# Weight parts of a feed-forward made by casting and accumulating DMAs instead of ScalarE and VectorE

## The chip, the cores and the metric

The kernel runs on one core of a Trainium2 chip. The metric is the device time of one execution in microseconds (us); less is better. Engines are named as in the profile: PE (matmul), PEld (its weight load), DVE (VectorE), ACT (ScalarE), POOL (GpSimd), SP (which issues the ordinary DMAs).

## The reference

An encoder layer is applied to two groups of 256 tokens of width 1024, with shared weights: layer norm, three branches (mLSTM, grouped-query attention with rotary positions, cross-attention to 256 memory tokens), a gated merge, an output projection with residual and norm, and a gated convolutional feed-forward with residual and norm. All is float32. The part that the change touches:

```python
def conv_ffn(x, w_ffn_up, ffn_conv_w, ffn_conv_b, w_ffn_down):
    u = dwconv_centred(x @ w_ffn_up, ffn_conv_w, ffn_conv_b)
    return (jax.nn.gelu(u[..., :D_FF]) * u[..., D_FF:]) @ w_ffn_down
```

`D_FF` is 2816, so `w_ffn_up` is 1024 x 5632 and `w_ffn_down` 2816 x 1024.

## The kernel before, in words

All 512 tokens are worked on at once; a PSUM tile is 128 x 512 float32. Every operand of a product is split into a high part and a low part in the matmul's format (float32r): the high part is the value cast to it, the low part is the value less the high part. A product is made of three matmuls: high by high, high by low, low by high (`mm3`, L120 to L122).

Weights come in chunks of 128 x 1024 (512 KB). A chunk is loaded by a DMA of the SP queue into one of three `raw` buffers (L95). ACT casts `raw` into `whi` (L108), DVE subtracts: `wlo = raw - whi` (L109). There are six `whi` and six `wlo` buffers (`NW`), taken in turn. For `w_ffn_up` a chunk is 8 pieces of 128 columns side by side, one for each k tile, and so in memory 1024 rows of 512 B; for `w_ffn_down` it is 128 rows of 4 KB.

The feed-forward has 22 blocks of 128 channels (`NF`), each with two up tiles, `ua` (gelu) and `ub` (gate). An up tile is 24 matmuls of 512 columns into one PSUM tile, out of four for dense products (`pd`). Then ACT reads the PSUM tile (L465) and DVE reads it twice (L468, L471) for the convolution over tokens; ACT applies gelu to `ua` (L1079); DVE multiplies the two into `hf` (L1083). The tiles of the first two blocks are made early, in two halves; the rest, 40 tiles, follow in order. The down product then runs over the 22 blocks; each chunk takes 24 matmuls into eight PSUM tiles at once (L1133 to L1135), and the split of `hf` into `hs` high and low (L82, L83) belongs to it. The last four blocks are done token tile by token tile, with the second norm between.

The code asks for chunks up to three jobs ahead (`LOOKAHEAD`). Each engine has its own list of instructions, whose order is fixed when the program is built; an engine that waits at one instruction does nothing behind it. Across engines only semaphores order the work.

Of the kernel before, what the change touches and what calls it, by code (L numbers as in the profile page):

```python
# [12 lines left out]
F32 = mybir.dt.float32  # L13
F32R = mybir.dt.float32r
# [7 lines left out]
T = 256            # tokens of one request group  # L22
NT = 512           # tokens of both groups
NTT = NT // P
HM = 4             # mLSTM heads
HA = 8             # attention heads
HC = 4             # cross-attention heads
# [7 lines left out]
MAX_EXP = 88.7      # its exponential is still finite  # L35

# columns of w_in
# [9 lines left out]
class Encoder:  # L47
# [27 lines left out]
    def split(self, src, name, scale=None):  # L75
        """src = hi + lo exactly, both with 12 significant bits."""
        nc = self.nc
        hi, lo = self.a(f"{name}h", F32R), self.a(f"{name}l", F32R)
        n = src.free_size()
        h, l = hi[:, :n], lo[:, :n]  # L80
        if scale is None:
            nc.scalar.copy(h, src)  # L82
            nc.vector.tensor_tensor(l, src, h.bitcast(F32), op=ALU.subtract)  # L83
        else:
            nc.scalar.activation(h, src, AF.Copy, scale=scale)
            nc.vector.scalar_tensor_tensor(
                l, src, scale, h.bitcast(F32), op0=ALU.mult, op1=ALU.subtract
            )
        return hi, lo
# [21 lines left out]

    def rsqrt(self, out, in_):
        self.nc.gpsimd.tensor_tensor(  # L113
            out, in_, self.mhalf.to_broadcast(list(in_.shape)), op=ALU.pow
        )

# [7 lines left out]
    def stat(self, chunk, sub, x, evac, name, k0=0):  # L124
        """A job: out[128 columns of w, tokens] = w.T x; chunk() gives w's parts."""

        def run():
            wh, wl = chunk()
            ps = self.ps(name, dense=True)
            nk = wh.shape[1]  # L130
            c = slice(sub * P, sub * P + P)
            for k in range(nk):
                xh, xl = x[k0 + k]
                self.mm3(ps, wh[:, k, c], wl[:, k, c], xh, xl, k == 0, k == nk - 1)
            evac(ps)

        return run

    def chunk(self, *args):
        return Chunk(self, args)  # L140

    def add_stat(self, w, c0, ntile, x, evac, name):
        nk = len(x)
        per = max(1, 1024 // (nk * P))
        for i in range(ntile):
            if i % per == 0:
                ch = self.chunk(w, 0, nk, c0 + i * P, per * P)
            self.jobs.append(([ch], self.stat(ch.get, i % per, x, lambda p, i=i: evac(i, p), f"{name}{i}")))

    def add_nat(self, w, c0, ncol, x, evac, name):  # L150
        """Jobs for out[tokens, ncol columns], accumulated over chunks of two k tiles."""
        nk = len(x)
        box = {}
        for c in range(nk // 2):
            ch = self.chunk(w, 2 * c, 2, c0, ncol)

            def run(c=c, ch=ch):
                wh, wl = ch.get()
                for t in range(NTT):
                    if c == 0:  # L160
                        box[t] = self.ps(f"{name}{t}", dense=True)
                    ts = slice(t * P, t * P + P)
                    for kk in range(2):
                        k = 2 * c + kk
                        xh, xl = x[k]
                        mm = self.nc.tensor.matmul
                        o = box[t][:, :ncol]
                        mm(o, xh[:, ts], wh[:, kk, :], start=(k == 0), stop=False)  # L168
                        mm(o, xh[:, ts], wl[:, kk, :], start=False, stop=False)  # L169
                        mm(o, xl[:, ts], wh[:, kk, :], start=False, stop=(k == nk - 1))  # L170
                    if c == nk // 2 - 1:
                        evac(t, box[t])

            self.jobs.append(([ch], run))
# [11 lines left out]
    def run_jobs(self):  # L186
        """Runs the jobs (the chunks that they use, run) in order, with the chunks made ahead
        as the pool lets, and the side steps spread between them."""
# [26 lines left out]
    def constants(self):  # L215
# [11 lines left out]
        # masks over [s, t]: forward keeps s <= t, backward s >= t  # L227
# [10 lines left out]
    def late_constants(self):  # L238
        """Per-channel vectors as columns, and the rotary tables with the norm gains in them."""
# [14 lines left out]
        # head norm gain, with the halves of the output gate's sigmoid and of the merge gates'  # L254
# [31 lines left out]
    def norm_stats(self, y, tag="ln", bufs=2, st=None):  # L286
        """[mean, variance, -, 1 / deviation] of the rows y."""
        nc = self.nc
        if st is None:
            st = self.sm([P, 2, 6], "lnst")  # L290
            for h in range(2):
                nc.vector.bn_stats(st[:, h, :], y[h])
        mv = self.sm([P, 4], f"{tag}mv", bufs)
        nc.vector.bn_aggr(mv[:, 0:2], st.rearrange("p a b -> p (a b)"))
        nc.vector.tensor_scalar(mv[:, 2:3], mv[:, 1:2], EPS, None, op0=ALU.add)  # L295
        self.rsqrt(mv[:, 3:4], mv[:, 2:3])
        return mv

    def layer_norm(self, y, gb, st=None, share=False):
        """share: the second half on ScalarE and GpSimd."""  # L300
# [25 lines left out]
    def gain_rows(self, y, gb, halves=(0, 1)):  # L326
        """Gain and bias of rows, where nothing waits for them."""
# [15 lines left out]
    def turn_part(self, rows, ts, out, name, fs=(0, KT), affine=None):  # L343
        """Parts of the transpose of some adjacent token tiles, into out[k tile]; affine:
        the columns of gains and biases to apply."""
# [32 lines left out]
    def attend(self, heads, qparts, kparts, v, hT):  # L378
        """Steps for some heads over both groups, as a pipeline of (head, group) units.
        qparts(h) makes and kparts(h) gives parts of the transposed queries and keys,  # L380
        v(h, g, kt) parts of [128 keys, 128]; parts of 0.5 * the output, transposed, go to hT."""
# [103 lines left out]
    def ev_vog(self, b):  # L485
        """Blocks of 384 | 328 | 328 of the columns v 512 | o 512 | g 16."""
        def f(t, ps):
# [11 lines left out]
            # forward gates beside zeros, and zeros beside backward gates  # L499
# [14 lines left out]
    def mlstm_steps(self, qk, hT):  # L514
        """qk[i]: twice silu of the convolved q (i < 4) and k heads, [128, tokens]."""
# [4 lines left out]
        def rows():  # L520
            # gate rows by (direction, head), each in its own direction's time order
# [10 lines left out]
            # scans restart at each chunk  # L532
# [20 lines left out]
            # the running maximum, less bl  # L553
# [3 lines left out]
            # weights into the state (first chunk) and of the state (second chunk)  # L557
# [26 lines left out]
        def flipped():  # L584
# [8 lines left out]
            # the negated maximum as rows by (tile, direction, head), for all partitions  # L593
# [6 lines left out]
        def colq(q, d, t):  # L600
            """[128, 4 heads] of quantity q, direction d, token tile t."""
# [78 lines left out]
        def out(t, h):  # L680
            g, c = t // 2, t % 2
            ds = 0 if c == 1 else 1     # the direction with a state before this chunk
# [74 lines left out]
    def ev_rope(self, parts):  # L757
        """parts: (column, heads, table, sink, (mul, add)) of a natural block."""
# [45 lines left out]
    def build(self):  # L804
# [34 lines left out]
        # memory keys and values  # L839
# [17 lines left out]
        with self.tc.manual_schedule(engines=engines):  # L857
            # the tensor engine is kept busy, so that its clock is up, until the first rows arrive
# [54 lines left out]
        # cross-attention queries, attention inputs  # L913
# [57 lines left out]
        # merge of the branches, one branch at a time  # L971
# [20 lines left out]
        def branch(n, w, hT, nk, first, last, name, flush=False):  # L992
# [6 lines left out]
            if flush:  # L999
                # the first gates cover the last steps of what the branch waits for  # L1000
# [12 lines left out]
        # mLSTM inputs  # L1013
# [24 lines left out]
        # output projection, first residual and norm  # L1038
# [31 lines left out]
        # gated convolutional feed-forward  # L1070
# [15 lines left out]
        # the first tiles of the product for one group while the other group's rows are made  # L1086
# [29 lines left out]
        for f in range(EARLY, NF):  # L1116
            if f == NF - 1:
                self.add(lambda: [down_split(z) for z in range(3)])
            self.add_stat(w_up, f * P, 1, x2s, ev_up(f, 0), f"ua{f}")
            self.add_stat(w_up, DFF + f * P, 1, x2s, ev_up(f, 1), f"ub{f}")  # L1120
# [16 lines left out]
        dn = [self.chunk(w_dn, f, 1, 0, D) for f in range(NF)]  # L1137
# [38 lines left out]
class Chunk:  # L1176
    """Parts of a block of weights (w, first k tile, k tiles, first column, columns), made once."""

    def __init__(self, enc, args):
        self.enc, self.args, self.raw, self.parts = enc, args, None, None  # L1180

    def load(self):
        if self.raw is None:
            self.raw = self.enc.load_chunk(*self.args)

    def get(self, pieces=1):
        if self.parts is None:
            self.load()
            self.parts = self.enc.split_chunk(self.raw, self.args[2], self.args[4], pieces)
# [4 lines left out]
class LazyPair:  # L1194
    """The parts of a tile that is made later."""
# [22 lines left out]
def _rope_table():  # L1218
    """[token, (cos, sin), dim], the sines signed for x * cos + swapped x * sin."""
# [30 lines left out]
```

## Time and profile before

| | us |
|---|---|
| times of two executions | 953.58, 955.25 |
| median | 954.41 |
| profiled execution: span from first to last instruction | 951.1 |
| what lies around the span, by the two times | 2.5 to 4.1 |
| PE busy in it | 937.3 (99%) |
| DVE busy | 555.5 (58%) |
| ACT busy | 377.9 (40%) |
| POOL busy | 106.8 (11%) |

The profile is one execution. Its page gives no time of its own for it beside the span, so the span stands against the two times. A busy PE means that a matmul is in its pipeline; matmuls overlap, so the distance between their starts tells their rate, not the length of one. A stage is read by its own window, not by the shares of the whole span. The stages here: late up tiles (blocks 10 to 21, 24 tiles) from 693 to 823 us, down product from 823 us to the end.

### The profile page before, as it was taken

The page shows a single profiled execution, that of the slowest core. Times are in us where ns is not written, and L with a number is a line of the kernel's source. Part 1 is how long each engine was busy: PE and PEld are TensorE (multiplying, and loading weights), DVE is VectorE, ACT ScalarE, POOL GpSimd, SP SyncE. Part 2 cuts the span into 40 slices and gives each one's busy share as a digit, 9 for nine tenths or more (in the row PEclk, how much of TensorE's full clock was granted, in tenths as well). Part 3 has the DMA queues.
Part 4 walks back from the last instruction along what each step waited for, and adds up shares of the span by engine and source line. Part 5 has one row for each costly group of instructions (what it writes and reads, how often), then busy time and mean ns, then how long its engine had stood idle before and what let it go on. Part 6 is the DMA issues. An engine that isn't in the chain of part 4 may idle for free.

```text
span 951.1 us, 12119 instructions
## 1 busy us (share of the span) xinstructions
PE 937.3 (99%) x4654; PEld 795.3 (84%) x4654; DVE 555.5 (58%) x1006; ACT 377.9 (40%) x677; POOL 106.8 (11%) x99
## 2 busy tenths in 40 slices
PE   9989999999999999999999999999999999999996
PEld 7878888888889997888878889988888888888885
DVE  4674444896777435457668567755555555752217
ACT  4652543434555444344344313533433333542101
POOL 0160100440000000111019001000000000000004
PEclk9999999999999999999999999999999999999998
DMA  8354223224111253432253523333333333242202
GB/s 291 100 163 114 85 67 89 72 63 132 51 46 44 68 141 92 143 99 78 80 201 97 155 67 89 111 90 110 89 93 107 89 106 94 89 155 89 88 1 89
DMA packets 121485, 95.76 MB, mean 101 GB/s; under 512 B 3664, under 2 KB 105812, under 8 KB 121428
## 3 DMA queue, kind: packets, MB, share of 16 engines
q1 hardware_dynamic: 121428, 94.99, 33.1%
q8 instruction: 37, 0.61, 0.3%
q14 instruction: 20, 0.16, 0.1%
HBM read 92.86 MB, written 2.11 MB: 100 GB/s over the span
## 4 chain that ended last, share of the span: by engine, by line
PE 87%; DVE 3%; POOL 2%; issue 0%; DMA 0%; ACT 0%; DVEq 0%; POOLq 0%; SPq 0%; ACTq 0%
PE dn L1135 4%; PE dn L1133 4%; PE dn L1134 4%; PE ua L120 4%; PE ub L120 4%; PE ua L121 4%; PE ub L121 4%; PE ub L122 4%; PE ua L122 4%; PE ga L120 2%; PE vog L169 2%; PE vog L170 2%; PE vog L168 2%; PE ga L121 2%; PE ba L120 2%; PE ga L122 2%
## 5 line engine op out<-in xcount | busy, mean ns | idle before, releaser
L109 DVE TENSOR_TENSOR wlo<-raw,whi 128x1024 fp32r<-128x1024 f32 (+3 forms) x162 | 194.9, 1206 | 274.5 <-ACT whi L108 274.3
L108 ACT CAST whi<-raw 128x1024 fp32r<-128x1024 f32 (+3 forms) x162 | 163.2, 1012 | 360.3 <-PE ua L121 72.0
L113 POOL TENSOR_TENSOR lnmv<-lnmv,mhalf 128x1 f32<-128x1 f32 x8 | 7.7, 965 | 403.5 <-DVE lnmv L295 403.5
L400 ACT ACTIVATE prob<-sc,nmax 128x256 f32<-128x256 f32 x48 | 22.5, 476 | 24.6 <-DVE nmax L396 24.5
L113 POOL TENSOR_TENSOR rss<-rss,mhalf 128x4 f32<-128x4 f32 (+1 forms) x12 | 22.3, 1859 | 75.9 <-DVE rss L779 75.9
L1079 ACT ACTIVATE up<-up 128x512 f32<-128x512 f32 x22 | 13.9, 633 | 42.4 <-DVE up L471 42.4
L329 POOL TENSOR_TENSOR y<-y,gain 128x512 f32<-128x512 f32 x11 | 18.4, 1678 | 15.8 <-ACT y L319 15.8
L396 DVE TENSOR_REDUCE nmax<-sc 128x2 f32<-128x512 f32 x24 | 16.4, 681 | 4.3 <-PE sc L122 4.3
L330 POOL TENSOR_TENSOR y<-y,gain 128x512 f32<-128x512 f32 x11 | 17.3, 1579 | 0.5
L83 DVE TENSOR_TENSOR probTl<-pt,probTh 128x512 fp32r<-128x512 f32 x24 | 16.4, 682 | 1.4 <-ACT probTh L82 1.4
L1083 DVE TENSOR_TENSOR hf<-up 128x512 f32<-128x512 f32 x22 | 15.2, 692 | 0.9
L465 ACT ACTIVATE up<-ub,col 128x512 f32<-128x512 f32 x20 | 15.6, 778 | 0.0
L465 ACT ACTIVATE up<-ua,col 128x512 f32<-128x512 f32 x20 | 15.5, 777 | 0.0
L986 DVE SCALAR_TENSOR_TENSOR gate<-gate,ba 128x512 f32<-128x512 f32 x8 | 5.5, 686 | 17.2 <-PE ba L122 9.2
L471 DVE SCALAR_TENSOR_TENSOR up<-ub,col,up 128x510 f32<-128x510 f32 x20 | 15.0, 748 | 0.7
L471 DVE SCALAR_TENSOR_TENSOR up<-ua,col,up 128x510 f32<-128x510 f32 x20 | 15.0, 748 | 0.7
L406 DVE TENSOR_SCALAR prob<-prob,rsum 128x256 f32<-128x256 f32 x48 | 14.8, 351 | 0.8
L82 ACT CAST probTh<-pt 128x512 fp32r<-128x512 f32 x24 | 14.0, 583 | 2.4 <-PE pt L417 1.9
L468 DVE SCALAR_TENSOR_TENSOR up<-ua,col,up 128x510 f32<-128x510 f32 x20 | 14.9, 743 | 0.0
L468 DVE SCALAR_TENSOR_TENSOR up<-ub,col,up 128x510 f32<-128x510 f32 x20 | 14.9, 743 | 0.0
L417 PE MATMUL pt<-ident,prob 128*128 128x128 f32 x96 | 14.7, 274 | 0.0
L319 ACT ACTIVATE y<-y,lnmv 128x512 f32<-128x512 f32 x3 | 2.4, 816 | 27.7 <-DVE lnmv L322 27.7
(1460 smaller groups left out, 2953.3 us busy)
## 6 DMA issues: line engine op xcount, KB each, us to landing
raw<-in_w_in SPq DMA_DIRECT2D x48, 512.0 KB
raw<-in_w_ffn_up SPq DMA_DIRECT2D x44, 512.0 KB
raw<-in_w_ffn_down SPq DMA_DIRECT2D x22, 512.0 KB
raw<-in_w_mem_kv SPq DMA_DIRECT2D x8, 512.0 KB
raw<-in_w_branch_attn SPq DMA_DIRECT2D x8, 512.0 KB
raw<-in_w_out SPq DMA_DIRECT2D x8, 512.0 KB
raw<-in_w_in SPq DMA_DIRECT2D x8, 328.0 KB
raw<-in_w_branch_mem SPq DMA_DIRECT2D x4, 512.0 KB
```

Source lines behind the costliest of these rows:

```text
L108: nc.scalar.copy(hi[:, s], raw[:, s])
L109: nc.vector.tensor_tensor(lo[:, s], raw[:, s], hi[:, s].bitcast(F32), op=ALU.subtract)
L113: self.nc.gpsimd.tensor_tensor(out, in_, self.mhalf.to_broadcast(list(in_.shape)), op=ALU.pow)
L120: mm(ps, lh, rh, start=first, stop=False)
L121: mm(ps, lh, rl, start=False, stop=False)
L122: mm(ps, ll, rh, start=False, stop=last)
L465: nc.scalar.activation(y, ps, AF.Identity, bias=w[3], scale=w[1])
L468: nc.vector.scalar_tensor_tensor(y3[:, :, 1:T], p3[:, :, 0 : T - 1], w[0], y3[:, :, 1:T], op0=ALU.mult, op1=ALU.add)
L471: nc.vector.scalar_tensor_tensor(y3[:, :, 0 : T - 1], p3[:, :, 1:T], w[2], y3[:, :, 0 : T - 1], op0=ALU.mult, op1=ALU.add)
L1133: mm(o, xh[:, ts], wh[:, 0, cs], start=(f == 0), stop=False)
L1134: mm(o, xh[:, ts], wl[:, 0, cs], start=False, stop=False)
L1135: mm(o, xl[:, ts], wh[:, 0, cs], start=False, stop=(f == NF - 1))
```

## The change

Two other ways to make a chunk's parts are added, and a chunk is told which one it uses.

- `cast`, for the up tiles of blocks 10 to 21 (24 chunks): a DMA of the POOL queue loads the weights from memory straight into `whi`, cast on the way. ACT writes `wlo = -whi`. A second DMA of the POOL queue reads the same weights from memory again and adds them into `wlo`. No `raw` buffer is used.
- `sum`, for all 22 down chunks: SP loads `raw` as before, ACT casts it into `whi` and writes `wlo = -whi`, and a DMA of the POOL queue adds `raw` into `wlo`, from on-chip memory to on-chip memory.

All other chunks are made as before. Comments and docstrings are dropped too, and the line numbers of what stands behind the new functions grow by 30.

```diff
+    def cast_chunk(self, w, k0, nk, c0, ncol):
+        n = nk * ncol
+        hi = self.whl.tile([P, 1024], F32R, tag="hi", name="whi")
+        lo = self.whl.tile([P, 1024], F32R, tag="lo", name="wlo")
+        self.nc.gpsimd.dma_start(
+            hi[:, :n].rearrange("p (k c) -> p k c", k=nk), self.chunk_src(w, k0, nk, c0, ncol)
+        )
+        return hi, lo
+
+    def finish_cast(self, parts, w, k0, nk, c0, ncol):
+        nc = self.nc
+        hi, lo = [t[:, : nk * ncol] for t in parts]
+        nc.scalar.activation(lo, hi.bitcast(F32), AF.Copy, scale=-1.0)
+        view = lambda t: t.rearrange("p (k c) -> p k c", k=nk)
+        nc.gpsimd.dma_start(view(lo), self.chunk_src(w, k0, nk, c0, ncol), accum_op=ALU.add)
+        return [view(t) for t in (hi, lo)]
+
+    def sum_chunk(self, raw, nk, ncol):
+        nc = self.nc
+        n = nk * ncol
+        hi = self.whl.tile([P, 1024], F32R, tag="hi", name="whi")
+        lo = self.whl.tile([P, 1024], F32R, tag="lo", name="wlo")
+        nc.scalar.copy(hi[:, :n], raw[:, :n])
+        nc.scalar.activation(lo[:, :n], hi[:, :n].bitcast(F32), AF.Copy, scale=-1.0)
+        nc.gpsimd.dma_start(lo[:, :n], raw[:, :n], accum_op=ALU.add)
+        return [t[:, :n].rearrange("p (k c) -> p k c", k=nk) for t in (hi, lo)]
...
-            self.add_stat(w_up, f * P, 1, x2s, ev_up(f, 0), f"ua{f}")
-            self.add_stat(w_up, DFF + f * P, 1, x2s, ev_up(f, 1), f"ub{f}")
+            self.add_stat(w_up, f * P, 1, x2s, ev_up(f, 0), f"ua{f}", "cast" if f >= 10 else "vec")
+            self.add_stat(w_up, DFF + f * P, 1, x2s, ev_up(f, 1), f"ub{f}", "cast" if f >= 10 else "vec")
...
-        dn = [self.chunk(w_dn, f, 1, 0, D) for f in range(NF)]
+        dn = [self.chunk(w_dn, f, 1, 0, D, how="sum") for f in range(NF)]
...
     def get(self, pieces=1):
         if self.parts is None:
             self.load()
-            self.parts = self.enc.split_chunk(self.raw, self.args[2], self.args[4], pieces)
+            if self.how == "cast":
+                self.parts = self.enc.finish_cast(self.raw, *self.args)
+            elif self.how == "sum":
+                self.parts = self.enc.sum_chunk(self.raw, self.args[2], self.args[4])
+            else:
+                self.parts = self.enc.split_chunk(self.raw, self.args[2], self.args[4], pieces)
```

In POOL's list nothing stood between the norms before the feed-forward and those of the tail. Now, at the start of the late up chunks (numbers tell buffers apart; L119 is the casting DMA, L129 the accumulating one):

```order
L143 TENSOR_TENSOR lnmv_5467<-lnmv_5467,mhalf_91 128x1
L119 DMA whi_6233<-in_w_ffn_up 128x8x128
L129 DMA wlo_6234<-in_w_ffn_up 128x8x128
L119 DMA whi_6269<-in_w_ffn_up 128x8x128
L129 DMA wlo_6270<-in_w_ffn_up 128x8x128
L119 DMA whi_6304<-in_w_ffn_up 128x8x128
L119 DMA whi_6340<-in_w_ffn_up 128x8x128
L129 DMA wlo_6305<-in_w_ffn_up 128x8x128
L129 DMA wlo_6341<-in_w_ffn_up 128x8x128
L119 DMA whi_6375<-in_w_ffn_up 128x8x128
L129 DMA wlo_6376<-in_w_ffn_up 128x8x128
```

From the third chunk on the pattern cast, cast, add, add, cast, add repeats to the last up chunk; then the 22 adds of the down chunks (L139) follow one another.

ACT's list at the same place before (L108 the cast of a chunk, L465 the read of an up tile's PSUM, L1079 gelu):

```order
L1079 ACTIVATE up<-up 128x512
L108 CAST whi<-raw 128x1024
L465 ACTIVATE up<-ub_6166,col 128x512
L108 CAST whi<-raw 128x1024
L465 ACTIVATE up<-ua_6203,col 128x512
L1079 ACTIVATE up<-up 128x512
```

and now (L127 the negation, L495 and L1109 what L465 and L1079 were):

```order
L1109 ACTIVATE up<-up 128x512
L127 ACTIVATE wlo<-whi 128x1024
L495 ACTIVATE up<-ub_6166,col 128x512
L127 ACTIVATE wlo<-whi 128x1024
L495 ACTIVATE up<-ua_6203,col 128x512
L1109 ACTIVATE up<-up 128x512
```

The negation stands where the cast stood, one chunk for one up tile; it now waits for the landing of the cast DMA of the chunk that is used six tiles after the tile read just before it.

## Rows read from the trace of the kernel before

**Rows 1.** Page: span, busy us and shares; the clock in 40 slices, in tenths.

```profile
span 951.1 us, 12119 instructions
...
PE 937.3 (99%) x4654; PEld 795.3 (84%) x4654; DVE 555.5 (58%) x1006; ACT 377.9 (40%) x677; POOL 106.8 (11%) x99
...
PEclk9999999999999999999999999999999999999998
```

**Rows 2.** Waits of PE: waiting line, releaser, us in total, times, longest; all.

```profile
PE xT3p L357 <- ACT affine L367: 1.6, 2, 1.0
PE warm L861 <- POOL ident masks.py:199: 1.5, 1, 1.5
PE hmT L736 <- DVE hm L729: 1.1, 1, 1.1
PE qc L121 <- POOL xT37l L375: 0.7, 1, 0.7
PE sc L122 <- DVE qTl L83: 0.3, 1, 0.3
PE mT1p L357 <- DMA mem<-in_mem_prompt: 0.3, 1, 0.3
PE qc L121 <- POOL xT36l L375: 0.2, 1, 0.2
```

**Rows 3.** Windows: late up stage, and down stage up to the last chunk made.

```profile
core 0: us, PE busy (x) PEld busy (x) DVE busy (x) ACT busy (x) POOL busy (x), PEclk, DMA share, GB/s
693.00:823.00 130.00, 130.00 (x576) 107.66 (x575) 73.31 (x87) 50.56 (x63) 0.00 (x0) 1.00 0.32 98
823.00:910.00 87.00, 87.00 (x385) 72.09 (x384) 33.13 (x38) 27.43 (x36) 0.00 (x0) 1.00 0.29 97
```

**Rows 4.** Lines, 693 to 823 us: line, out<-in, count; busy us, mean ns; idle before.

```profile
L109 DVE TENSOR_TENSOR wlo<-raw,whi 128x1024 fp32r<-128x1024 f32 x24 | 29.4, 1225 | 56.0 <-ACT whi L108 56.0
L108 ACT CAST whi<-raw 128x1024 fp32r<-128x1024 f32 x24 | 25.3, 1055 | 54.4 <-PE ua L121 43.0 <-PE ub L121 11.5
L465 ACT ACTIVATE up<-ua,col 128x512 f32<-128x512 f32 x12 | 9.3, 777 | 0.0
```

**Rows 5.** Timeline: start us, us; one up tile from first to last matmul, next.

```profile
703.76 0.39 PE L120 MATMUL ua<-x2T0h,whi 128*128 128x512 f32 x1
...
708.98 0.39 PE L122 MATMUL ua<-x2T7h,wlo 128*128 128x512 f32 x1
709.21 0.39 PE L120 MATMUL ub<-x2T0h,whi 128*128 128x512 f32 x1
...
709.18 1.05 ACT L108 CAST whi<-raw 128x1024 fp32r<-128x1024 f32 x1 [3.71 <-PE ua L121]
```

**Rows 6.** Source line L1135: one kind of matmul in two adjacent down chunks.

```profile
L1135 PE MATMUL dn<-whi,hs0l x8: 389/389/389, 823.9 to 828.7; 128*128 128x512 f32 x8
...
L1135 PE MATMUL dn<-whi,hs1l x8: 389/389/389, 829.3 to 834.1; 128*128 128x512 f32 x8
```

**Rows 7.** Waits of ACT and SP; tile raw: SP's issues, ns min/median/max.

```profile
ACT whi L108 <- PE ua L121: 72.0, 20, 3.7
...
SPq L95 <- DVE wlo L109: 697.5, 137, 11.6
...
L95 SPq DMA_DIRECT2D raw<-in_w_ffn_up x44: 367/368/379, 538.5 to 776.8; - x44
```

**Rows 8.** Chain of waits, 210 to 222 us: a load waited for.

```profile
215.11 3.83 DMA raw<-in_w_in
219.02 1.06 ACT whi L108
```

**Rows 9.** Lines of POOL.

```profile
L329 POOL TENSOR_TENSOR y<-y,gain 128x512 f32<-128x512 f32 x11 | 18.4, 1678 | 15.8 <-ACT y L319 15.8
...
L113 POOL TENSOR_TENSOR lnmv<-lnmv,mhalf 128x1 f32<-128x1 f32 x8 | 7.7, 965 | 403.5 <-DVE lnmv L295 403.5
```

**Rows 10.** Lines of ACT, 823 to 910 us.

```profile
L82 ACT CAST hs4h<-hf 128x512 fp32r<-128x512 f32 x1 | 0.6, 624 | 0.0
```

More of the change, by code (lines that the diff above doesn't have):

```diff
@@ L110, in split_chunk, with chunk_src @@
         return [t[:, :n].rearrange("p (k c) -> p k c", k=nk) for t in (hi, lo)]
+    def chunk_src(self, w, k0, nk, c0, ncol):
+        return w[k0 * P : (k0 + nk) * P, c0 : c0 + ncol].rearrange("(k p) c -> p k c", p=P)
+    def cast_chunk(self, w, k0, nk, c0, ncol):
[22 more added lines that the diff above has]
+        return [t[:, :n].rearrange("p (k c) -> p k c", k=nk) for t in (hi, lo)]
     def rsqrt(self, out, in_):
@@ L137, in stat, with chunk, add_stat @@
         return run
-    def chunk(self, *args):
-        return Chunk(self, args)
-    def add_stat(self, w, c0, ntile, x, evac, name):
+    def chunk(self, *args, how="vec"):
+        return Chunk(self, args, how)
+    def add_stat(self, w, c0, ntile, x, evac, name, how="vec"):
         nk = len(x)
@@ L146, in add_stat @@
             if i % per == 0:
-                ch = self.chunk(w, 0, nk, c0 + i * P, per * P)
+                ch = self.chunk(w, 0, nk, c0 + i * P, per * P, how=how)
             self.jobs.append(([ch], self.stat(ch.get, i % per, x, lambda p, i=i: evac(i, p), f"{name}{i}")))
@@ L1176, with __init__ @@
 class Chunk:
-    def __init__(self, enc, args):
-        self.enc, self.args, self.raw, self.parts = enc, args, None, None
+    def __init__(self, enc, args, how="vec"):
+        self.enc, self.args, self.how, self.raw, self.parts = enc, args, how, None, None
     def load(self):
         if self.raw is None:
-            self.raw = self.enc.load_chunk(*self.args)
+            if self.how == "cast":
+                self.raw = self.enc.cast_chunk(*self.args)
+            else:
+                self.raw = self.enc.load_chunk(*self.args)
     def get(self, pieces=1):
@@ L1188, in get @@
             self.load()
-            self.parts = self.enc.split_chunk(self.raw, self.args[2], self.args[4], pieces)
+            if self.how == "cast":
+                self.parts = self.enc.finish_cast(self.raw, *self.args)
+            elif self.how == "sum":
+                self.parts = self.enc.sum_chunk(self.raw, self.args[2], self.args[4])
+            else:
+                self.parts = self.enc.split_chunk(self.raw, self.args[2], self.args[4], pieces)
             self.raw = True
```

## The prediction

> **What bounds the kernel now.** I read the page's busy shares first, then the waits of PE, then the two stages that the change touches, then single instructions in them.
>
> PE is busy for 99% of the span, at a granted clock of nine tenths or more in all slices but the last [rows 1]. All the waits of PE together are about 6 us, none of them in the feed-forward [rows 2]. In the stage of the late up tiles (693 to 823 us) and in that of the down product (from 823 us) PE is busy the whole time at clock 1.00, DVE for 73.3 of 130 us, ACT for 50.6, POOL not at all, and the DMA engines for 0.32 of the time [rows 3]. One up tile is 24 matmuls in 709.21 - 703.76 = 5.45 us, one down chunk 829.3 - 823.9 = 5.4 us [rows 5, 6]. So the weights are prepared beside PE, and nothing that makes preparing cheaper can shorten the time. The change can lose time or leave it.
>
> What keeps PE fed is early preparation. There are six buffers for high and low parts, and the ACT cast of a late tile begins when the tile six before it has been read: at 709.18 us, where the last matmul of such a tile started at 708.98 [rows 5]; the waits of ACT name this releaser 20 times [rows 7]. So a tile has five tile lengths, 5 x 5.45 = 27.2 us, from free buffer to first use. Before, the preparation takes 1.06 us on ACT and 1.23 us on DVE [rows 4] with the load already there: over 24 us to spare.
>
> **The change, part by part.**
>
> *Removed.* 46 DVE subtractions (24 in the late up stage, 22 in the down product) of 1.23 us each [rows 4], some 56 us of DVE; and 24 loads of the SP queue. DVE is not waited for there, so 0 us.
>
> *Moved.* ACT keeps one pass of 1.06 us per late up tile (now a negation in place of a cast) and gets a second one per down chunk: 2 x 1.06 + 0.62 for the split of the other operand = 2.7 us of 5.4 [rows 4, 10]. Hidden, 0 us.
>
> *Added on the late up tiles: a chain through POOL's queue.* Per tile: cast DMA (512 KB from HBM), negation on ACT, accumulating DMA (512 KB from HBM again). POOL runs them in a fixed order, with a period of three tiles: cast, add, cast, cast, add, add. An add waits for ACT, and ACT for the landing of the cast; every cast behind that add waits as well. So POOL makes two round trips per three tiles, and PE gives it 3 x 5.45 = 16.3 us. I need four durations.
> - A plain transfer: 98 GB/s over 130 us are 12.7 MB, 24.3 chunks of 524 KB, in 0.32 x 130 = 41.6 us of all DMA engines, so 1.71 us each [rows 3]. I take it for the cast too.
> - Latency: the one plain load that the chain of waits shows bare took 3.83 us from issue to use [rows 8], so 2.1 us beside the transfer; I put half before and half behind it.
> - The issue on POOL: no row shows one. Below stands SP's issue of the same shape, 0.37 us [rows 7]; above, POOL handling one element per lane in 1678/512 = 3.3 ns, which for the transfer's 1024 pieces of 512 B is 3.4 us [rows 9]. I take 1.0 us, near POOL's shortest steps of software, 0.97 us for one element [rows 9], and keep 0.37 and 3.4 as ends.
> - The accumulating transfer: no row shows one. Below, a plain transfer, 1.71 us. Above, three of them, 5.13 us, if reading the source, reading the target and writing do not overlap. I take two, 3.42 us: two reads where the plain one has one, with the writing hidden as it is there.
>
> The Trainium skill, "Collectives: The Full Stack", section on the bandwidth ceiling, says that an add in a DMA costs no cycles for the adding but needs two source reads, with a measured ratio of 1.93; by that alone (an estimate) the sum below would be 29 in place of 32 us. No row of this trace shows it.
>
> Now the period, from the moment POOL is done with the previous pair of adds. These still fill the DMA engines until 6.2 us (both issued within 1.7 us, 2 x 3.42 to move, latency ahead). First cast: issued at 1.0, moves 6.2 to 7.9, lands at 9.0. Negation (1.06 and 0.1 of hand-over): 10.1. Its add issued at 11.1. Two casts issued at 12.1 and 13.1. The add moves 12.2 to 15.6, the casts to 17.3 and 19.0, landing at 18.4 and 20.1. Negations at 19.5 and 21.2, adds issued at 20.5 and **22.2 us**. So a period takes 22.2 and not 16.3: 5.9 us are lost every three tiles, over 24 tiles 8 x 5.9 = 47 us. What is in hand is 27.2 less one unhindered chain, 1.0 + 3.8 + 1.15 + 1.0 + 5.5 = 12.5, so 14.7 us. PE then waits 47 - 15 = **32 us**.
>
> The DMA engines themselves are not full: (1.71 + 3.42) x 3 = 15.4 of 16.3. The round trips leave gaps in which nothing is queued.
>
> The Trainium skill, "DMA: Bandwidth & Descriptors", section on the anatomy of one DMA, gives 2.0 us + bytes/436e3, so 3.2 us for 512 KB, and calls descriptor generation small. The bare load above took 3.83 us, so the measurement is used; with 3.2 us the period would be 21.0 us (an estimate).
>
> *ACT behind the landing.* ACT's queue has the negation of tile n ahead of the PSUM read of tile n-5, so a late cast also delays evacuation. There are four PSUM buffers, so PE needs that read only for tile n-1; this binds at about the same lateness as the add, and I add nothing.
>
> *Added on the down chunks.* One add from SBUF per chunk. A plain load there is 0.29 x 87 us for 16.1 chunks, 1.57 us [rows 3]; with an add of two, 1.57 + 3.14 = 4.7 us of 5.4. The raw buffers (three) are held until the add lands: 3.8 load + 2.2 ACT + 1.0 + 5.3 = 12.3 us, a third of it 4.1 us per chunk. Both fit: 0 us. SP's loads wait for that landing where they waited for DVE [rows 7].
>
> **Sum.** Against the profiled execution: span 951.1 us [rows 1] + 32 = 983; the two runs lie 2.5 to 4.1 us above that span, so against their median of 954.4 it is **987 us**, 3.4% slower.
>
> **The rivals.**
> - *Hidden: PE never waits.* An add at a plain transfer's price gives, by the same steps, a period of 17.1 us: 8 x 0.8 = 6 us, under the 14.7 in hand. At one and a half transfers it is 19.7, and 12 us are lost, still within 2%. For it: over 24 us to spare today and DMA engines idle two thirds of the time [rows 3]. Against: POOL's order. Time 950 to 973, at best 954. Chance 0.30. It decides the other way from about 1.7 transfers on.
> - *The add is dear.* At three transfers the period is 27.4 us: 8 x 11.0 - 15 = 73 us, and the down stage is over as well, 1.57 + 4.71 = 6.3 of 5.4 us, 22 x 0.85 = 19 us. Time 1046; at four transfers about 1120. Chance 0.18.
> - *The issue on POOL is the bound.* At 3.4 us per issue six of them are 20.4 us by themselves and the period is 27.0 even with a cheap add: 8 x 10.7 - 15 = 71 us, 1025. It begins to decide at 2.7 us. Chance 0.11.
> - *Faster.* The matmuls would have to come closer together once DVE reads SBUF less. Against: 5.45 us per tile with DVE at 73.3/130 and 5.4 with it at 33.1/87 [rows 3, 5, 6]. At most the 6 us of waits in all [rows 2], outside the change. More than 2% is next to excluded: 0.03.
>
> **How the numbers follow.** My forecast (add of 1.7 to 2.6 transfers, issue under 2.7 us, time 973 to 1015) has 0.38. A change within 2% (19 us) is about what can't be told from none. Slower by more: 0.38 + 0.18 + 0.11 = 0.67; same 0.30; faster 0.03. The range begins at 950, for the hidden case, and ends at 1062: it takes in three transfers with issues at 1.9 us (period 29.1, 87 + 19 us), and leaves out an add of four and the like. For the forecast alone it is 970 to 1020.
>
> **What would show it.** In the late up stage PE's busy share falls to about 0.8, its waits name a DMA into the low parts, and tiles come 7 us apart from about the seventh on, not from the first; the down stage stays at 5.4 us per chunk. POOL's issues about 1 us, adds at twice a plain transfer in the DMA share. PE without waits in both stages would show the first rival right; waits in the down stage, the second; issues near 3 us, the third.

## The result, and the profile after

The changed kernel takes **1007.34 us** (1006.38 and 1008.3) against 954.41: a ratio of 1.0553, 95% interval 1.052 to 1.0586. The forecast was 987, in a range of 950 to 1062. The profiled execution of the changed kernel is the 1008.3 one.

The page, with the lines that answer to [rows 1], and the DMA slices:

```profile
span 1006.5 us, 12180 instructions
...
PE 958.1 (95%) x4654; PEld 806.5 (80%) x4654; DVE 502.5 (50%) x960; ACT 398.7 (40%) x699; POOL 184.6 (18%) x169
...
PEclk9999999999999999999999999999988888899998
DMA  7353222242211433333525134349899999799842
```

PE was idle for 951.1 - 937.3 = 13.8 us before and is for 48.4 now: 34.6 us more, next to the forecast 32. But its busy time has grown too, by 20.8 us, though it runs the same 4654 matmuls. Slices 30 to 35 of the clock show where: the granted clock falls in the late up stage and at the start of the down product. That busy time looks like a second loss beside the idle time; the last experiment below shows that it is not one.

The windows that answer to [rows 3]: six of POOL's periods, the rest of the late up stage with the first down chunk, and nine later down chunks. Columns as there.

```profile
696.00:835.70 139.70, 115.12 (x453) 91.44 (x452) 32.88 (x46) 36.17 (x45) 44.26 (x37) 0.90 0.98 135
835.70:880.00 44.30, 35.87 (x130) 28.05 (x129) 14.43 (x21) 19.65 (x25) 9.96 (x10) 0.85 0.85 154
919.50:968.50 49.00, 49.00 (x218) 40.59 (x217) 0.00 (x0) 19.04 (x18) 7.75 (x10) 1.00 0.84 190
```

In the late up stage PE is busy for 0.82 and 0.81 of the time, at clock 0.90 and 0.85. In the down product it is busy all the time at clock 1.00, 49.00 / 9 = 5.44 us per chunk, as before.

POOL's timeline over two of its periods (start, length, line, output; L119 casts, L129 adds; a row of x2 holds two issues):

```profile
696.00 1.57 POOL L119 DMA_DIRECT2D whi<-in_w_ffn_up  x1
705.79 1.54 POOL L129 DMA_DIRECT2D wlo<-in_w_ffn_up  x1 [8.22 <-ACT wlo L127]
706.68 2.46 POOL L119 DMA_DIRECT2D whi<-in_w_ffn_up  x2
716.46 1.57 POOL L129 DMA_DIRECT2D wlo<-in_w_ffn_up  x1 [7.31 <-PE ub L151]
720.45 1.56 POOL L129 DMA_DIRECT2D wlo<-in_w_ffn_up  x1 [2.43 <-ACT wlo L127]
721.35 1.57 POOL L119 DMA_DIRECT2D whi<-in_w_ffn_up  x1
730.35 1.54 POOL L129 DMA_DIRECT2D wlo<-in_w_ffn_up  x1 [7.43 <-ACT wlo L127]
731.26 2.43 POOL L119 DMA_DIRECT2D whi<-in_w_ffn_up  x2
740.03 3.15 POOL L129 DMA_DIRECT2D wlo<-in_w_ffn_up  x2 [6.34 <-ACT wlo L127]
742.49 1.60 POOL L119 DMA_DIRECT2D whi<-in_w_ffn_up  x1
```

This is the chain of the forecast: two round trips of 9 to 10 us per three tiles, POOL idle in them and every later cast queued behind the waiting add. The periods are 25.35 and 21.14 us; over six of them (696.00 to 835.73) the mean is 23.3, where 22.2 was forecast and PE's pace is 16.3.

ACT in the same stretch tells why long and short periods alternate:

```profile
715.09 1.06 ACT L127 ACTIVATE wlo<-whi 128x1024 fp32r<-128x1024 f32 x1 [8.94 <-DMA whi<-in_w_ffn_up]
716.06 0.76 ACT L495 ACTIVATE up<-ua,col 128x512 f32<-128x512 f32 x1
718.48 0.63 ACT L1109 ACTIVATE up<-up 128x512 f32<-128x512 f32 x1 [1.66 <-DVE up L501]
719.01 1.04 ACT L127 ACTIVATE wlo<-whi 128x1024 fp32r<-128x1024 f32 x1
...
728.77 1.06 ACT L127 ACTIVATE wlo<-whi 128x1024 fp32r<-128x1024 f32 x1 [8.05 <-DMA whi<-in_w_ffn_up]
729.74 0.76 ACT L495 ACTIVATE up<-ua,col 128x512 f32<-128x512 f32 x1
732.16 0.63 ACT L1109 ACTIVATE up<-up 128x512 f32<-128x512 f32 x1 [1.66 <-DVE up L501]
738.58 1.06 ACT L127 ACTIVATE wlo<-whi 128x1024 fp32r<-128x1024 f32 x1 [5.80 <-DMA whi<-in_w_ffn_up]
739.55 0.76 ACT L495 ACTIVATE up<-ub,col 128x512 f32<-128x512 f32 x1
740.24 1.06 ACT L127 ACTIVATE wlo<-whi 128x1024 fp32r<-128x1024 f32 x1
```

The negations of a pair of casts are 1.66 us apart where the read of a `ub` tile stands between them (738.58, 740.24), and 3.92 where that of a `ua` tile does (715.09, 719.01): then the gelu, which waits for two passes of DVE, stands ahead of the second negation as well. These 2.3 us are about half of the 4.2 by which the periods differ; the rest lies in POOL's trips from cast to add, 9.79 and 9.78 us in the long period, 9.00 and 8.77 in the short one, and why is open.

Where PE stops. The timeline at the first matmul of some late tiles, with what DVE does ahead of one of them (other rows left out):

```profile
711.08 0.39 PE L150 MATMUL ub<-x2T0h,whi 128*128 128x512 f32 x1
...
718.48 0.47 PE L150 MATMUL ua<-x2T0h,whi 128*128 128x512 f32 x1 [1.80 <-issue]
...
731.32 0.75 DVE L501 SCALAR_TENSOR_TENSOR up<-ua,col,up 128x510 f32<-128x510 f32 x1
...
732.16 0.77 PE L150 MATMUL ua<-x2T0h,whi 128*128 128x512 f32 x1 [2.53 <-issue]
...
741.98 0.77 PE L150 MATMUL ub<-x2T0h,whi 128*128 128x512 f32 x1 [2.75 <-ACT up L495]
```

PE resumes at 732.16, 0.09 us after DVE has ended the last read of a PSUM tile (731.32 + 0.75 = 732.07). That read follows ACT's at 729.74, and ACT's stood behind the negation at 728.77, which had waited 8.05 us for a cast to land. So PE waits for a PSUM buffer, through ACT's list. The view names it badly: "issue", or ACT, which had been done for a while.

The waits of PE from 690 to 890 us (line, releaser, us in total, times, longest), which answer to [rows 2]:

```profile
PE ua L150 <- issue: 13.1, 5, 4.3
PE ub L150 <- ACT up L495: 11.2, 3, 4.3
PE dn L1163 <- ACT hs0h L82: 4.4, 1, 4.4
PE ua L150 <- ACT whi L137: 3.8, 1, 3.8
```

Together 32.5 us (two more rows of 0.5 us in all are left out), and no DMA into a low part among them.

### The profile page after: what moved, and what is told of

Its sections match the earlier page's. It is cut to its first block, busy times and chain, and to the rows that moved or that the text cites. A ratio compares the mean times of both kernels' runs of the same rounds, so it can differ in the third digit from the quotient of the medians.

```text
span 1006.5 us, 12180 instructions
## 1 busy us (share of the span) xinstructions
PE 958.1 (95%) x4654; PEld 806.5 (80%) x4654; DVE 502.5 (50%) x960; ACT 398.7 (40%) x699; POOL 184.6 (18%) x169
## 4 chain that ended last, share of the span: by engine, by line
PE 73%; issue 9%; POOL 4%; DVE 3%; DMA 2%; ACT 1%; DVEq 0%; POOLq 0%; SPq 0%; ACTq 0%
PE dn L1165 4%; PE dn L1163 4%; PE dn L1164 4%; PE ua L150 2%; PE ua L151 2%; PE ua L152 2%; PE ub L151 2%; PE ub L150 2%; PE ub L152 2%; POOL whi L119 2%; PE ga L150 2%; PE vog L199 2%; PE vog L200 2%; PE vog L198 1%; PE ga L151 1%
## 5 line engine op out<-in xcount | busy, mean ns | idle before, releaser
L109 DVE TENSOR_TENSOR wlo<-raw,whi 128x1024 fp32r<-128x1024 f32 (+3 forms) x116 | 139.9, 1210 | 149.8 <-ACT whi L108 149.5
L108 ACT CAST whi<-raw 128x1024 fp32r<-128x1024 f32 (+3 forms) x116 | 114.6, 995 | 231.5 <-PE ga L151 27.3
L127 ACT ACTIVATE wlo<-whi 128x1024 fp32r<-128x1024 f32 x24 | 25.3, 1056 | 117.7 <-DMA whi<-in_w_ffn_up 117.7
L498 DVE SCALAR_TENSOR_TENSOR up<-ub,col,up 128x510 f32<-128x510 f32 x20 | 15.0, 748 | 95.5 <-ACT up L495 95.5
L129 POOL DMA_DIRECT2D wlo<-in_w_ffn_up x24 | 37.4, 1560 | 130.7 <-ACT wlo L127 123.2
L119 POOL DMA_DIRECT2D whi<-in_w_ffn_up x24 | 32.5, 1549 | 79.3 <-PE ua L152 79.3
L498 DVE SCALAR_TENSOR_TENSOR up<-ua,col,up 128x510 f32<-128x510 f32 x20 | 14.9, 746 | 63.6 <-ACT up L495 63.6
L137 ACT CAST whi<-raw 128x1024 fp32r<-128x1024 f32 x22 | 23.1, 1049 | 48.3 <-PE dn L1165 34.3
L139 POOL DMA_DIRECT2D wlo<-raw x22 | 18.9, 858 | 92.6 <-ACT wlo L138 92.6
L1109 ACT ACTIVATE up<-up 128x512 f32<-128x512 f32 x22 | 13.9, 631 | 34.1 <-DVE up L501 34.0
L150 PE MATMUL ua<-x2T0h,whi 128*128 128x512 f32 x20 | 9.5, 476 | 16.9 <-issue 13.1
L138 ACT ACTIVATE wlo<-whi 128x1024 fp32r<-128x1024 f32 x22 | 23.2, 1056 | 0.4
```

What stands on the lines that cost most here:

```text
L108: nc.scalar.copy(hi[:, s], raw[:, s])
L109: nc.vector.tensor_tensor(lo[:, s], raw[:, s], hi[:, s].bitcast(F32), op=ALU.subtract)
L119: self.nc.gpsimd.dma_start(hi[:, :n].rearrange("p (k c) -> p k c", k=nk), self.chunk_src(w, k0, nk, c0, ncol))
L129: nc.gpsimd.dma_start(view(lo), self.chunk_src(w, k0, nk, c0, ncol), accum_op=ALU.add)
L150: mm(ps, lh, rh, start=first, stop=False)
L498: nc.vector.scalar_tensor_tensor(y3[:, :, 1:T], p3[:, :, 0 : T - 1], w[0], y3[:, :, 1:T], op0=ALU.mult, op1=ALU.add)
```

## The experiments

The theory **W**: POOL's order makes PE wait, two round trips for three tiles. Rivals: the DMA engines are full; the accumulating DMA is too dear; the lower granted clock is a loss of its own.

**Half of the change each.** Only the down chunks the new way (L1149, L1150):

```diff
-... f"ua{f}", "cast" if f >= 10 else "vec")
+... f"ua{f}", "vec")
```

> Only the down chunks are made the new way; the up tiles are as before. Both theories (POOL's order; full DMA engines): a down chunk asks the DMA engines for 0.84 x 49 / 9 = 4.6 us of 5.44, and its chain has room, so nothing is lost: 954 us, within 4. If the 51.8 us by which the first down chunk is late in the changed kernel were in part the down chunks' own doing, 960 or more.

Measured: 953.64, ratio 0.9996 (0.9984 to 1.0007). Its window that answers to [rows 3]:

```profile
823.00:910.00 87.00, 87.00 (x386) 72.06 (x385) 14.36 (x23) 44.56 (x53) 14.14 (x17) 1.00 0.86 206
```

PE is full at a DMA share of 0.86 where it was 0.29. The 0 us forecast for the down chunks holds.

Only the late up chunks:

```diff
-        dn = [self.chunk(w_dn, f, 1, 0, D, how="sum") for f in range(NF)]
+        dn = [self.chunk(w_dn, f, 1, 0, D) for f in range(NF)]
```

> Only the late up tiles are made the new way; the down chunks are as before. Both theories: nearly the whole loss, 47 us by the last up tile, so 1000 us; the 4.4 us wait and the 3 us of lower clock at the first down chunk may go: 998 to 1007. POOL's period of three tiles stays at 23.3 us.

Measured: 1003.59, ratio 1.0512 (1.049 to 1.0533). All but about 4 us of the loss is here.

**The add's price.** As the last one, but the second DMA does not accumulate; the low parts then are the weights themselves:

```diff
-        nc.gpsimd.dma_start(view(lo), self.chunk_src(w, k0, nk, c0, ncol), accum_op=ALU.add)
+        nc.gpsimd.dma_start(view(lo), self.chunk_src(w, k0, nk, c0, ncol))
```

> As the run with the casts alone, but the second DMA of a late up tile casts and does not add (the low parts are then the weights themselves, so the output is not the reference's). It prices the adding. Theory 1 (POOL's order, two round trips per three tiles): the trips stay and only the queueing behind adds shrinks; period 18 to 21 us, loss 12 to 30 us, time 966 to 984. Theory 2 (the engines are full with 7.6 us per pair): a pair of casts is 5 to 6 us, about what PE takes (5.45); loss 0 to 12 us, 954 to 966. If adding costs the DMA engines nothing, both: as with the add, about 1000.

Measured: 973.88, ratio 1.0199 (1.0173 to 1.0225). The DMA issues from 693 to 823 us (KB each, median us from issue to landing), of the kernel ahead of it, then of this one:

```profile
wlo<-in_w_ffn_up POOLq DMA_DIRECT2D x18, 512.0 KB, 6.3
whi<-in_w_ffn_up POOLq DMA_DIRECT2D x18, 512.0 KB, 8.2
```

```profile
wlo<-in_w_ffn_up POOLq DMA_DIRECT2D x19, 512.0 KB, 4.6
whi<-in_w_ffn_up POOLq DMA_DIRECT2D x19, 512.0 KB, 6.3
```

Without the accumulation the second DMA lands 1.7 us sooner, just the 1.71 by which the forecast had priced it above a plain transfer. POOL's period is 19.6 us (691.15 to 789.28 are five). So even an add at a plain cast's price leaves a period over 16.3 in this order. The price counts, since it lies in the round trip: 49 us are lost with the accumulation (1003.59) and 19 without it. But it takes this order for it to cost anything, as the next run shows.

**The order of POOL's list.** As the cast-only kernel, but with POOL's list kept in program order, and each cast issued up to five jobs ahead of its chunk's use, which is two tiles ahead of its add: add, cast, add, cast, with two other casts between a cast and its own add.

```diff
+            for j in range(i + 1, min(i + AHEAD, len(jobs) - 1) + 1):   # AHEAD = 5
+                for c in jobs[j][0] or ():
+                    if c.how == "cast":
+                        c.load()
...
-        self.run_jobs()
+        with self.tc.manual_schedule(engines={mybir.EngineType.Pool}):
+            self.run_jobs()
```

> As the run with the casts alone, with the same DMAs, but POOL's list alternates cast and add, each add two or three casts behind its own, so that POOL never waits for the landing of the DMA it has just issued. Theory 1 (POOL's order sets the period): the period falls to what PE takes, 16.3 us; time 954 to 962, PE without waits. Theory 2 (DMA engines full, 7.6 us per pair): the period stays at 21 us or more; 985 to 1005.

Measured: **954.17**, ratio 0.9998 (0.9987 to 1.0008): the whole loss is gone, with the same DMAs. Its window of the late up stage, and POOL's wait:

```profile
693.00:823.00 130.00, 130.00 (x575) 107.65 (x574) 51.64 (x68) 51.02 (x64) 50.00 (x40) 1.00 1.17 184
```

```profile
POOL whi L120 <- PE ua L153: 116.3, 13, 68.4
```

PE is full at clock 1.00. POOL now waits for buffers that PE frees, and for ACT only twice (7.1 us in all). The DMA engines move 184 GB/s here against 135 in the changed kernel, whose share of 0.98 was thus no limit; the share goes over 1 in this kernel, which keeps pace. An add takes longer here, 7.5 us to land in the median, and costs nothing.

The other end: the same code with `AHEAD = 0`, so that each add follows its own cast.

> As the run with the casts alone, but POOL's list is cast, add, cast, add throughout: one round trip per tile in place of two per three tiles, with the same DMAs. In the changed kernel such a single trip, from one cast's issue to the next, takes 731.26 - 721.35 = 9.9 us. Theory 1 (POOL's order): 24 x (9.9 - 5.45) - 11 in hand = 96 us lost, 1035 to 1055. Theory 2 (full DMA engines): no more queued at a time than before, 1000 to 1010.

Measured: 1043.71, ratio 1.0938 (1.0913 to 1.0963). Three round trips for three tiles. Here PE does wait for the low part:

```profile
PE ua L153 <- DMA wlo<-in_w_ffn_up: 27.5, 9, 4.2
PE ub L153 <- DMA wlo<-in_w_ffn_up: 21.7, 9, 3.1
```

**What is in hand.** The changed kernel with the cast for the last four blocks alone, 8 tiles (`f >= 18` for `f >= 10`):

> The changed kernel with the new way for the last 8 up tiles in place of 24; the down chunks as there. What is in hand before PE has to wait: by the forecast 14.7 us, so 8 tiles lose 8/3 x 7.0 - 14.7 = 4 us: 957 to 960. By the changed kernel's trace, where the eighth late tile starts 9.1 us late, and the first down chunk waits and is slow for some 7 us more: 963 to 972.

Measured: 967.55, ratio 1.0138 (1.0117 to 1.0158). The time lies in the second range, but the trace doesn't bear out its terms. The eight tiles start 4.2 us late (784.13 for 779.92), without a wait of PE from 690 us on to there. The eighth starts 9.2 us late (827.22 for 818.00), so only 5.0 us are lost in the stage, nearer to the 4 of the forecast than to 9.1. The second down chunk starts 16.0 us late (844.84 for 828.88), so 6.8 are lost at the first one. The forecast's range left out that loss, and so this run doesn't tell 14.7 us in hand from less.

**The clock.** Where a tile waits, its first matmuls run slowly (0.77 us at 732.16 for 0.39). Two kernels should make PE pause without any DMA of POOL: the kernel before, with POOL making the late low parts from `raw`, slowed by repeating the subtraction. First evenly:

```diff
+        parts = [(0, 1024), (0, 1024), (0, 256)]
+        for c0, c in parts:
+            s = slice(c0, c0 + c)
+            nc.gpsimd.tensor_tensor(lo[:, s], raw[:, s], hi[:, s].bitcast(F32), op=ALU.subtract)
```

> The kernel before, but the low parts of the late up tiles are made by POOL, by subtraction, and written 2.25 times over so that POOL takes about 7.3 us per tile (from 3.2 us per 1024 columns, by 1.6 per 512 in the trace). No casting or accumulating DMA is left. PE must wait some 2 us in nearly every tile. Theory W (the clock falls because PE pauses): the clock falls below 1.00 in that stage. Theory D (it falls with the traffic of POOL's DMAs): it stays at 1.00. Time 24 x (7.3 - 5.45) - 16 = 28 us over, 975 to 990, in both.

Then unevenly:

```diff
-        parts = [(0, 1024), (0, 1024), (0, 256)]
+        parts = [(0, 1024)] * (5 if self.nslow % 3 == 2 else 1)
```

> As the run with even pauses, but POOL writes the low part once for two tiles and five times for the third: 22.4 us per three tiles, so one pause of some 6 us per three tiles. Theory W: the clock falls further, to 0.85 or below in the stage, with slow matmuls right behind each pause; PE's busy time grows by 10 us or more over the kernel before. Theory D: clock 1.00 and PE's busy time as before, 937 us. Time 975 to 990 in both.

Measured: 956.09, ratio 1.0021 (1.0011 to 1.0032), and 962.21, ratio 1.0084 (1.0064 to 1.0104). Both missed: one subtraction took 2.46 to 2.51 us, so a chunk took 2 x 2.46 + 0.87 = 5.8 us or three took 17.6, and what is in hand covered nearly all of it. But in the second kernel PE does pause at the start of the down product, three times within 14 us: for 2.55, 1.6 and 1.9 us. Its PE timeline and windows there:

```profile
823.25 0.39 PE L166 MATMUL ub<-x2T7h,wlo 128*128 128x512 f32 x1
826.19 0.80 PE L1177 MATMUL dn<-whi,hs0h 128*128 128x512 f32 x1 [2.55 <-ACT hs0h L83]
826.79 0.63 PE L1178 MATMUL dn<-wlo,hs0h 128*128 128x512 f32 x1
```

```profile
824.00:830.00 6.00, 2.18 (x4) 1.34 (x5) 4.94 (x7) 4.80 (x8) 0.00 (x0) 0.67 0.30 110
830.00:836.00 6.00, 5.39 (x18) 3.98 (x16) 4.26 (x6) 3.14 (x5) 0.00 (x0) 0.76 0.24 87
```

After the first pause the granted clock is 0.67 and 0.76, mixtures of the two levels of 1.2 and 2.4 GHz, and matmuls run at 0.63 us, with POOL idle and a DMA share of 0.3 and 0.24. So the fall comes with the pause, and neither POOL nor its DMAs are needed for it. One place shows this.

Next, the changed kernel with the pauses filled: eight matmuls into a spare PSUM tile ahead of each late up tile.

```diff
+            for _ in range(fill):                       # 8
+                xh = list(x[0])[0]
+                self.nc.tensor.matmul(self.spare, xh[:, :P], xh, start=True, stop=True)
```

> The changed kernel with eight extra matmuls of 512 columns ahead of each late up tile, into an unused PSUM tile, some 24 x 1.8 = 43.6 us of PE. Theory W (PE's clock falls because PE pauses, and what it costs inside the stage is taken from the waits, since POOL sets the pace): the clock stays near 1.00 in the stage, the period stays 23.3 us, and the time is the same or up to 8 us less (the slow matmuls and the wait at the first down chunk): 999 to 1010. Theory A (the 21 us that the lower clock adds to PE's busy time are lost on top): 980 to 990. Theory N (the clock does not depend on PE's pauses): clock still near 0.87, and 1020 or more.

Measured: 1045.81, ratio 1.096 (1.0944 to 1.0976), outside every expectation. POOL's list tells why: with the added matmuls the scheduler had put it into the order add, cast, wait (rows of the trace, one tile apart).

```profile
725.81 1.56 POOL L121 DMA_DIRECT2D whi<-in_w_ffn_up  x1
734.93 1.54 POOL L131 DMA_DIRECT2D wlo<-in_w_ffn_up  x1 [7.55 <-ACT wlo L129]
735.84 1.54 POOL L121 DMA_DIRECT2D whi<-in_w_ffn_up  x1
```

That is the order of the `AHEAD = 0` kernel, and the two agree to 0.2% (1045.81 and 1043.71; the one with the fillers also has the down chunks the new way), though their windows from 693 to 880 us, this one first, differ in the clock by a tenth:

```profile
693.00:880.00 187.00, 162.59 (x674) 129.92 (x673) 36.19 (x50) 38.40 (x48) 47.16 (x39) 0.96 0.74 109
```

```profile
693.00:880.00 187.00, 139.71 (x504) 107.76 (x503) 41.46 (x57) 41.86 (x53) 47.99 (x40) 0.87 0.71 107
```

So the last run repeats the filling with POOL's list held to the changed kernel's own order:

```diff
+                    if c.how == "cast":
+                        c.load()
+                        self.late += 1
+                        if self.late % 3 == 0:
+                            for d in jobs[nxt + 1][0] or ():
+                                if d.how == "cast":
+                                    d.load()
                     c.get()
...
-        self.run_jobs()
+        with self.tc.manual_schedule(engines={mybir.EngineType.Pool}):
+            self.run_jobs()
```

> The changed kernel with eight filler matmuls ahead of each late up tile, as in the run before it with fillers, but with POOL's list held to the changed kernel's own order (cast, add, cast, cast, add, add), since there the fillers had turned it into cast, add, cast, add. The fillers keep PE at work, so its granted clock stays near 1.00. If POOL's round trips alone set the pace (23.3 us for three tiles in the changed kernel) and the lower clock only filled time in which PE would have waited, the time stays at 1000 to 1012 us with a clock above 0.95 in the late up stage. If the 20.8 us that PE's matmuls grew by at the lower clock are a loss of their own, they come back: 980 to 992. If the fillers hold back the buffers or the evacuations, the period grows past 24 us and the time past 1018.

Measured: **1007.22**, ratio 1.0557 (1.054 to 1.0575), the changed kernel's time. From 693 to 880 us, this kernel first, then the changed one:

```profile
693.00:880.00 187.00, 182.34 (x796) 149.93 (x795) 49.36 (x68) 60.22 (x76) 56.70 (x47) 0.99 0.94 140
```

```profile
693.00:880.00 187.00, 153.99 (x595) 121.98 (x594) 49.37 (x68) 58.27 (x74) 56.70 (x47) 0.89 0.93 138
```

PE is busy for 0.98 of that time at clock 0.99, has run 201 matmuls more (192 of them are the fillers), and the time is the same. POOL's issues stand within 1.6 us of where they stood all through the stage: 697.03 for 696.00, 721.37 for 721.35, 742.48 for 742.49, 846.21 for 847.37. POOL's list, with ACT's and DVE's work in its round trips, sets the time, whatever PE does in between; the lower clock filled time in which PE would have waited. The DMA share is the same too (0.94 and 0.93) while the clock differs, so the DMA traffic doesn't set the clock here.

**What is left to gain.** The whole change with the order add, cast (`AHEAD = 5` and the list kept, `how="sum"` for the down chunks):

> The whole change (late up and down chunks) with the alternating order of POOL's list. Theory 1: nothing is lost, 952 to 958; POOL's order was the whole of it. Otherwise, if the down chunks collide with the last adds, 958 to 965. It can't be faster than the kernel before, since PE doesn't wait there.

Measured: 955.03, ratio 1.0009 (0.9999 to 1.0019). And the changed kernel with the late up chunks made as the down chunks are (`"sum"` for `"cast"`):

> All chunks that the change touches are made the second way (SP loads the raw weights, ACT casts and negates, POOL's DMA adds from on-chip memory), in the scheduler's order; no casting DMA. POOL's list is then only adds, with one wait for ACT each and no round trip. Theory 1: no loss, 951 to 958, though the DMA engines carry as much. Theory 2 (traffic): 1.7 for the load and 3.0 for the add are 4.7 of 5.45 us, so 951 to 958 as well; above 965 neither holds.

Measured: 953.48, ratio 0.9997 (0.9986 to 1.0008). Neither beats the kernel before. PE was full there, and is full here.

## Why the prediction was right in its mechanism and 20 us short

**Right.** Nothing could be gained: the four kernels that free DVE without stopping PE lie within 0.1% of the kernel before. The loss comes from POOL's order, with the round trip of cast, negation and add in it: the same DMAs take 1043.71, 1003.59 or 954.17 us by the order of the list, with the lead over its add that it gives a cast. The prices were near. By the forecast's terms a bare cast takes 1.0 + 2.1 + 1.71 = 4.8 us from issue to landing; the shortest ones took 4.8 in the changed kernel and 4.4 without the accumulation. The add was put at 1.71 us more, so 6.5; it took 6.4 in the median. The forecast's sign in the DMA share, adds at twice a plain transfer, did not come out: a cast with its add took 0.98 x 139.7 / 18 = 7.6 us of it, for 5.1, and two casts, by the kernel without accumulation (1.03 from 693 to 823 us), 1.03 x 19.6 / 3 = 6.7. So a cast counts there for about 3.4 and an add for 4.2, where a plain load of the kernel before counts 1.71. Issues follow each other on POOL at 0.9 us (705.79, 706.68), forecast 1.0. Of the two rules of the Trainium skill weighed there, the ratio of 1.93 for an add ("Collectives: The Full Stack", section on the bandwidth ceiling) can't be read off the landings directly, but it would make an add dearer by 0.93 x 1.71 = 1.6 us (an estimate). The 1.7 us between accumulating and not are near that; by the share above an add is only 0.8 us dearer than a cast. The 3.2 us for a bare 512 KB ("DMA: Bandwidth & Descriptors", section on the anatomy of one DMA) is short of the 4.4 us measured here from issue to landing, of which POOL's issue is 0.88.

**Short by.** The time lies in the forecast's own 970 to 1020; that it lies in 950 to 1062 too says little, since that range took in the hidden case as well. The span grew by 1006.5 - 951.1 = 55.4 us, where the forecast had 32. The terms, from the traces:

| term | forecast us | measured us |
|---|---|---|
| period less PE's pace, times 8 | 8 x 5.9 = 47 | 8 x 7.0 = 56 |
| in hand before PE stops (measured: by difference) | -14.7 | -10.7 |
| start of the late up stage, 694.76 for 692.88 | 0 | 1.9 |
| wait at the first down chunk | 0 | 4.4 |
| that chunk run slowly, 9.0 us (875.22 to 884.22) for 5.4 | 0 | 3.6 |
| sum | 32 | about 55 |

- *The period* was the mis-sized term that weighed most, 9 us. The mean is 23.3 for 22.2. In the two periods shown the trip of the single cast is shorter than forecast (9.79 and 9.00 us from cast to add, for 10.1), that of the pair is longer (9.78 and 8.77, for 8.4), and the pair's adds lie 3.99 and 1.6 us apart, for 1.7. The 3.99 is the part that the traces explain: the forecast let ACT negate 0.1 us after a cast had landed, and in the long periods the gelu and DVE's two passes stand ahead of the second negation.
- *In hand.* The last late tile starts at 865.22 where it started at 818.00, so 47.2 us late; less the 1.9 us of the start, 45.3 of the 56 are seen there, and 10.7 were hidden. The run with 8 tiles gives 8/3 x 7.0 - 5.0 = 13.7 by the same difference, so the size stays open between the two. The step that failed is "binds at about the same lateness as the add, and I add nothing". PE stops for a PSUM tile behind a negation before it stops for a low part; the first pause, 1.80 us, comes at the fifth late tile (718.48). For the tile that starts at 741.98 the add was issued at 730.35 and, at the median of 6.4 us, had landed at about 736.8; its PSUM tile was read out at 741.88. The forecast also said that the waits would name a DMA into the low parts. They do so only in the `AHEAD = 0` kernel.
- *The start of the down product* was left out. ACT's list has the cast of a down chunk (L137) ahead of the last PSUM read and of the split of `hs0`, and now that cast waits for its load. The forecast checked the time for which a raw buffer is held (12.3 us) against the pace of later chunks, and not at the start: the first down add was issued at 858.88, behind the late stage, and landed at 865.14; only then was a raw buffer free for the load, which ran from 865.20 to 871.91. With the up tiles as before, the first down add is issued at 801.13, and nothing waits. The 4.4 us are in the waits above, and PE's first matmuls behind them run at 0.63 us.

```profile
858.88 0.89 POOL L139 DMA_DIRECT2D wlo<-raw  x1 [1.01 <-ACT wlo L138]
871.99 1.04 ACT L137 CAST whi<-raw 128x1024 fp32r<-128x1024 f32 x1 [6.41 <-DMA raw<-in_w_ffn_down]
```

- *The clock* was not forecast at all. It fell, and cost nothing in the late up stage, as the filled kernel shows. That the forecast idle time (32) and the measured (34.6) agree so well is in part chance: the loss is larger, and slow matmuls cover a part of it.

The 1.9 us at the start of the stage are there before the first cast DMA's tile is used. The kernel with the casts alone is the same up to the down product and starts the stage at 693.13; and in the profiled execution of the changed kernel PE waits 1.9 us in the first 100 us for the load of the memory tokens, where it waited 0.3 before. So they belong to the execution, not to the change.

The rivals. *Hidden* needed an add at a plain transfer's price and gave a period of 17.1 for it; the kernel without accumulation has 19.6 and takes 973.88, so in this order it is not hidden even then, and the steps of the forecast were 2.5 us per period short without any add in them. *The add is dear* and *the issue is the bound* fall with the prices above; the down stage never waited behind its first chunk.

## What to carry to other kernels

When work goes to a queue that runs in order, count the round trips in the list, not the transfers: an instruction that waits for its own predecessor's landing stops everything behind it, and two tiles' distance between a cast and its add was worth 5% here with the same bytes. Follow the new wait through every list that it enters, ACT's PSUM reads behind a negation in this case, since the first buffer to run out sets what is in hand. And look whether an idle engine's slow stretch costs anything before counting it: fill it, and see whether the end moves.

## What the hardware showed unexpectedly

- Issues on POOL overlap in the trace: the rows have 1.55 us for casts and adds, yet the next one starts 0.9 us after (705.79, 706.68). Without accumulation a cast's issue took 0.88 us in the median (873 to 1106 ns over 24).
- The page's DMA share went to 1.17 over 130 us in a kernel whose PE never waited, and 0.98 went with 49 GB/s less: the share is not a measure of what is left.
- Matmuls ran slowly for longer than PE had paused. In the unevenly slowed kernel PE paused for 2.55 us; from 826.19 on matmuls took 0.63 to 0.80 us, with a second pause of 1.6 us up to 829.04, and from 832.96 on 0.39 again. A third pause of 1.9 us, up to 837.28, was followed by one matmul of 0.47 us and then 0.39 again; the granted clock from 836 to 842 is 1.00, the level of 2.4 GHz. So not every pause of some 2 us brought the lower level.
